# Four projections at the last super-block boundary over 512 columns in two contraction halves, and a later release of one buffer in the planner

## The chip, the cores and the metric

The kernel runs on one core of a Trainium2 chip. The metric is device time in microseconds (us), lower is better; every time below is of that one core. The engines are PE (TensorE, matmuls; PEld is its weight load), DVE (VectorE), ACT (ScalarE), POOL (GpSimd) and SP (SyncE, which here issues nearly all DMAs).

## The reference

One step of a layer that mixes attention and a gated linear recurrence, for 2048 prompt rows and 64 sample rows of width 1024, all in float32:

```
xn = rms_norm(x, ln_g)                                  # 2112 rows x 1024
aq, ak, av, ag, hq, hf, hi, hg = split(xn @ w_in)       # w_in 1024 x 4096: 8 parts of 512
o_a = band_attention(aq, ak, av) * silu(ag)             # 8 heads of 64, chunks of 64 rows, 576 keys each
o_b, S = hgrn2(hq, hf, hi, lb, state)                   # 4 heads of 128, blocks of 16 rows
o_b = rms_norm(o_b, norm_g) * silu(hg)
y = rms_norm(x + concat(o_a, o_b) @ w_out, ln_f_g)      # also returned: new keys, values and states
```

## The kernel before, in words

The rows are worked in four **super-blocks** (`sb` 0 to 3) of 512, 576, 512 and 512 rows. For each, the normalized rows stand transposed in SBUF, as a high part `xh` and a low part `xl` (both of the reduced float32 form that PE takes at its fast rate), 8 tiles `kt` of the contraction by the block's columns. There is one such pair of tiles; the next super-block's rows overwrite it.

A super-block has 32 **jobs** (`JOBS`), numbered `u` within it and `j` over all: one 128-column group of `w_in` each (`hf`, `hq`, `hi`, `hg` of a recurrent head, `pg`, `pq`, `pk`, `pv` of a pair of attention heads). `project` does one: 24 matmuls per range of columns (high x high, high weight x low, low weight x high, each over 8 `kt`) into one of two PSUM banks `acc`. A generator `evac` then empties the bank on ACT and DVE. The weight pair `w` (4 buffers) comes from a copy in DRAM, `wd`.

**The boundary.** Between two super-blocks PE must go on while `xh` and `xl` are rewritten. So the last two jobs of a super-block, and the first two of the next, are done in halves of 256 columns: job, job, on columns 0 to 255, then both on 256 to 511. After the first half the flag `x_left[sb, 0]` is set, after the second `x_left[sb, 1]`. The threads `x_back` (one per 128 rows) wait for the flag of their half of the columns, then write `xh` (an ACT cast for each half `k0` of the contraction, line 468) and spawn `x_low`, which writes `xl` (a DVE subtraction, line 474). The rows come from DRAM, already normalized and transposed, into a tile `xn` or `wraw`. `x_ready` tells the projections of the next super-block what has been written.

The values of attention, projected by `pv`, go from `acc` through a DVE block transpose (line 767), four DMAs to DRAM (`way<-vT`, line 787) and one back (`vT<-way`, line 791), then an ACT cast and a DVE subtraction into `v` (lines 756 and 759).

**The order.** One class, `Plan`, runs the whole kernel as generators at build time. It holds a clock `C.now` that the matmuls move on, and a free time for each engine; each buffer is a token (`tk[...]`), and `put(n, t)` says from what planned time it counts as free. A thread goes on when its token and its time have come, and instructions are written in the order in which threads go on. That order is then fixed on each engine. A planned time that is too early does no harm to the data: the instruction waits on the chip, and everything behind it on its engine waits too.

**The output part.** After the jobs the output projection runs as seven products per two tiles of rows (`steps`). `out_parts` splits each operand into a high part (ACT, line 1918) and a low part (DVE, or POOL at line 1926) in one of five rooms, the `slot`s. One room is made of `ob` and `gg`, the tiles of the recurrence's last output. It may be written once the store of `ob` to DRAM (`mixd<-ob`, line 1750, in `rec_block`) has read it. The last lines of `rec_block` say when the plan believes that:

```
sp.dma_start(mixd[sb][4 + h, :, c], ob[:, :bn])
if lastb and (sb, h) == (len(SUPER) - 1, NHB - 1):
    tk["slot"].put(1, C.now + 4500.0)
```

In attention, PE transposes the probabilities into one of two PSUM banks `tr` (line 254), ACT copies the high part `ph` (line 1055), DVE subtracts for the low part (line 1058), which frees the bank, and PE multiplies with the values into `pv`.

Of the kernel before, what the change touches and what calls it, by code (L numbers as in the profile page):

```python
# [19 lines left out]
KT = D // P  # L20
# [22 lines left out]
]  # L43
NMAX = 576


JOBS = [[(k, g) for g in range(4) for k in ("hf", "hq", "hi", "hg", "pg", "pq", "pk", "pv")] for _ in SUPER]
# [137 lines left out]
def hymba_step(  # L185
# [38 lines left out]
    C = Plan()  # L224
# [9 lines left out]
    def acc_ps():  # L234
        return psum("acc", bufs=2)
# [13 lines left out]
    def mm(out, w, x, n, slow=False, **kw):  # L249
        pe.matmul(out, w, x, **kw)  # L250
        C.mm(n, slow)

    def transpose(out, x, idn):
# [4 lines left out]
                                     w=WBUFS, raw=RAWB, xn=XNB, kv0=1, kv1=1, rec=1, sga=2, bias0=1, bias1=1, gf=1, gi=1, gg=1,  # L258
# [67 lines left out]
    xh = T(px, [P, KT, NMAX], F32R, "xh")  # L326
    xl = T(px, [P, KT, NMAX], F32R, "xl")

# [123 lines left out]
    def x_back(sb, half, c, rows, room, t):  # L452
        yield lambda: job[0] >= (20 if sb < 3 else 24) and x_turned.get(sb, 0) == c // P
        yield t
        while not (tk["xn"].n or tk["raw"].n):
            yield min(tk["xn"].when(), tk["raw"].when(), C.now + 300.0)
        tag = "xn" if tk["xn"].n else "raw"
        tk[tag].take()
        x_turned[sb] = c // P + 1
        xn = T(px, [P, D], F32, "xn", bufs=XNB) if tag == "xn" else raw_tile().rearrange("p k n -> p (k n)")  # L460
        sp.dma_start(xn[:, : 8 * rows], room.rearrange("p a x -> p (a x)"))
        t = C.dma(512 * rows / P) + 1000.0
        src = xn[:, : 8 * rows].rearrange("p (a k i) -> p k a i", k=KT, i=32)
        hi, lo = (x[:, :, c : c + rows].rearrange("p k (a i) -> p k a i", i=32) for x in (xh, xl))
        for k0 in (0, 4):
            yield lambda: x_left.get((sb - 1, half), False)
            yield "A", t
            act.copy(hi[:, k0 : k0 + 4], src[:, k0 : k0 + 4])
            C.spawn(x_low(sb, half, k0, rows, hi, lo, src, tag, C.act(4 * rows, t)), 0)
# [31 lines left out]
    def x_ready(sb, half, part, k0):  # L501
        tiles = (SUPER[sb][3][half][1] + P - 1) // P
        n, t = x_there.get((sb, half, part, k0), (0, 0.0))
        return n == tiles and t <= C.now
# [57 lines left out]
    def out_weights():  # L562


        for a in range(4):
            for tag in ("raw", "raw", "xn", "xn"):
                yield from tk[tag].get()
            r0, r1 = (raw_tile().rearrange("p k n -> p (k n)") for _ in range(2))
            stage = [T(px, [P, D], F32, "xn", bufs=XNB) for _ in range(2)]
            sp.dma_start(r0, w_out[a * P : (a + 1) * P, :])  # L570
            sp.dma_start(r1, w_out[(a + 4) * P : (a + 5) * P, :])
            yield "A", C.dma(1024)
            b11, b12, b21, b22 = r0[:, :512], r0[:, 512:], r1[:, :512], r1[:, 512:]
            state = dict(n=0, t=C.now)
            cols = [slice(c, c + 256) for c in (0, 256)]

            def split(i, src):
                st = stage[state["n"] % 2]
                t = max(state["t"], state.get(state["n"] - 2, 0.0))
                state["n"] += 1  # L580
                for c in cols:
                    yield "A", t
                    act.copy(f32r(st[:, c]), src[:, c])  # L583
                    t = C.act(256, t)
                    yield "P", t
                    pool.tensor_sub(f32r(st[:, c.start + 512 : c.stop + 512]), src[:, c], st[:, c])  # L586
                    t = C.pool(320, t)
                sp.dma_start(wod[i][:, :, a], st.rearrange("p (h c) -> p h c", h=2))
                state["t"] = t
                state[state["n"] - 1] = C.dma(512, t) + 2000.0  # L590

            def minus(out, x, y):
                for c in cols:
                    yield "P", state["t"]
                    pool.tensor_sub(out[:, c], x[:, c], y[:, c])
                    state["t"] = C.pool(320, state["t"])

            yield from split(0, b11)
            yield from split(1, b21)
            yield from split(5, b22)  # L600
            yield from tk["ck"].get()
            t3 = T(wk, [P, 512], F32, "ck", bufs=1)
            yield from minus(t3, b22, b12)
            yield from split(4, t3)
            tk["ck"].put(1, state["t"])
            yield from minus(b12, b12, b11)
            yield from minus(b22, b22, b12)
            yield from minus(b21, b21, b22)
            for i, src in ((3, b12), (2, b22), (6, b21)):
                yield from split(i, src)  # L610
            for tag, n in (("raw", 2), ("xn", 2)):
                tk[tag].put(n, C.now + 4000.0)
            yield C.now + 6000.0

    def project(j, ranges, evac, close=True, ready=None):
        yield lambda: j in w_at
        w, th, tl = w_at[j]
        yield th
        if ready:
            yield lambda: ready(0, 0)  # L620
        for off, bn in ranges:
            yield from tk["acc"].get()
            acc = acc_ps()
            n = 0
            for i, (wi, x) in enumerate(((0, xh), (0, xl), (1, xh))):
                for kt in range(KT):
                    if i == 2 and kt % 2 == 0:
                        yield lambda: len(tl) > kt // 2
                        yield tl[kt // 2]
                    if ready and i < 2 and kt % 4 == 0:  # L630
                        yield lambda: ready(i, kt)
                    mm(acc[:, :bn], w[:, wi, kt, :], x[:, kt, off : off + bn], bn,
                       start=(kt == 0 and i == 0), stop=(kt == KT - 1 and i == 2))
                    n += 1
                    if n % 2 == 0:
                        yield None
            C.spawn(evac(acc[:, :bn], off, bn, C.pe()), 0)
        if close:
            tk["w"].put(1, C.pe())
# [832 lines left out]
    def rec_block(r, off, bn, lastb):  # L1472
# [276 lines left out]
        yield t  # L1749
        sp.dma_start(mixd[sb][4 + h, :, c], ob[:, :bn])  # L1750
        if lastb and (sb, h) == (len(SUPER) - 1, NHB - 1):
            tk["slot"].put(1, C.now + 4500.0)
        done_g[sb, h] = done_g.get((sb, h), 0) + bn


# [422 lines left out]
    def program():  # L2178
# [67 lines left out]
        for sb in range(nsb):  # L2246
            last = sb == nsb - 1
            halves = SUPER[sb][3]
            blocks = SUPER[sb][2]
            if sb == 2:  # L2250
                C.spawn(out_weights(), 0.7)
            made = {}
            for u, (kind, g) in enumerate(JOBS[sb]):
                job[:] = u, sb
                if u == len(JOBS[sb]) - (8 if last else 32):
                    if last:
                        C.spawn(out_load(0), 1.5)
                        C.spawn(out_load(1), 1.6)
                        for rows in (out_rows_w(), out_rows_g(), out_rows_x(), out_rows_a()):
                            C.spawn(rows, 2)  # L2260
                    else:
                        C.spawn(x_turn(sb + 1), 0.5)
                if (kind[0], g) not in made:
                    d, evs = made[kind[0], g] = (head_jobs if kind[0] == "h" else pair_jobs)(sb, g)
                    C.spawn((recurrence if kind[0] == "h" else attention)(d), 1)
                evac = made[kind[0], g][1][kind[1]]

                if u == 1 or (u == len(JOBS[sb]) - 1 and not last):
                    for half in range(2):
                        yield from project(j - 1, [halves[half]], before, half == 1,  # L2270
                                           lambda part, k0: x_ready(sb, half, part, k0))
                        yield from project(j, [halves[half]], evac, half == 1,
                                           lambda part, k0: x_ready(sb, half, part, k0))
                        if u > 1:
                            x_left[sb, half] = True
                elif u != 0 and (last or u != len(JOBS[sb]) - 2):
                    yield from project(j, blocks, evac)
                    if u == len(JOBS[sb]) - 1:
                        x_left[sb, 0] = x_left[sb, 1] = True
                before = evac  # L2280
                j += 1
# [166 lines left out]
```

## Time and profile before

| what | value |
|---|---|
| median of 3 runs | 1211.92 us (1209.15 to 1214.72) |
| the profiled execution | 1212.41 us, of which 1210.4 us are the profile's span |
| mean granted PE clock | 0.997 |
| PE busy | 1195.2 us (99%), 7796 matmuls |
| PEld busy | 1051.3 us (87%) |
| DVE busy | 899.9 us (74%) |
| ACT busy | 715.0 us (59%) |
| POOL busy | 438.6 us (36%) |

The page names PE as busy for nearly the whole span, and 82% of the chain that ended last is PE. Matmuls are pipelined and the profile models their ends, so a matmul's duration is longer than the distance to the next; the distance between starts is what one costs. The boundary that the change touches lies at about 757 to 788 us; the store of the recurrence's last output at 1003 to 1009 us.

### The profile page before, as it was taken

Reading aid. Unit: us, or ns where it says so; the run is one execution under the profiler, and the core shown is the slowest. Engines: PE = TensorE matmul, PEld = TensorE weight load, DVE = VectorE, ACT = ScalarE, POOL = GpSimd, SP = SyncE. Lnnn points to the kernel's source line nnn. Section 1 sums busy time; section 2 is a strip of 40 time slices with the busy share of each in tenths; the row PEclk is TensorE's granted clock in tenths of the full one; section 3 lists DMA queues with packets and bytes.
Section 4 is the critical chain, followed back from the end, with each engine's and each line's share of the span. In section 5 each row is a group of like instructions: output and inputs, shape, how many; then the busy total and the mean of one; then the engine's idle time right before and its main releaser. Section 6 shows DMA issues by size and latency. Waiting matters only on the chain.

```text
span 1210.4 us, 22192 instructions
## 1 busy us (share of the span) xinstructions
PE 1195.2 (99%) x7796; PEld 1051.3 (87%) x7796; DVE 899.9 (74%) x1891; ACT 715.0 (59%) x1584; POOL 438.6 (36%) x738
## 2 busy tenths in 40 slices
PE   9999999999999999999999999999999998999997
PEld 7888788999999999998888888988888887888786
DVE  7698978777858777687677876786757574877775
ACT  6464655656666565774656665756656563644443
POOL 7776656112121121200234341143331213465443
PEclk9999999999999999999999999999999999999999
DMA  9899989687566595578697998688986677787431
GB/s 349 315 354 326 321 302 363 227 252 245 180 196 210 179 307 159 189 263 278 207 328 245 304 317 297 213 282 287 284 300 226 205 256 238 297 293 212 144 126 69
DMA packets 164696, 306.87 MB, mean 254 GB/s; under 512 B 49705, under 2 KB 102697, under 8 KB 146922
## 3 DMA queue, kind: packets, MB, share of 16 engines
q1 hardware_dynamic: 164152, 305.20, 74.5%
q8 instruction: 61, 1.00, 0.3%
q14 instruction: 49, 0.40, 0.1%
q10 hardware_dynamic: 434, 0.27, 0.1%
HBM read 204.75 MB, written 101.71 MB: 253 GB/s over the span
## 4 chain that ended last, share of the span: by engine, by line
PE 82%; DMA 5%; DVE 5%; ACT 4%; SPq 2%; issue 1%; POOL 1%; ACTq 0%; DVEq 0%; POOLq 0%
PE acc L250 53%; PE pv L250 7%; PE g L250 6%; PE s L250 5%; PE tr L254 5%; PE tr L250 4%; DMA xn<-in_x_prompt_dram 1%; DMA wraw<-in_w_in_dram 1%; PE g L1468 1%; SPq L445 1%; DMA carry<-kd 1%; DMA far<-in_rel_bias_dram 0%; DMA mixd<-ob 0%; ACT q L878 0%; DMA xn<-xt 0%
## 5 line engine op out<-in xcount | busy, mean ns | idle before, releaser
L250 PE MATMUL acc<-xh,w 128*128 128x512 f32 (+2 forms) x2720 | 564.1, 347 | 1.2 <-DVE sga L656 0.6
L250 PEld LDWEIGHTS acc<-xh,w 128*128 128x128 f32 x2720 | 436.2, 189 | 52.7 <-DVE sga L656 1.5
L250 PE MATMUL acc<-xl,w 128*128 128x512 f32 (+2 forms) x1360 | 290.8, 346 | 0.5 <-DVE xl L491 0.5
L250 PEld LDWEIGHTS acc<-xl,w 128*128 128x128 f32 x1360 | 220.5, 189 | 25.2 <-DVE xl L491 0.7
L1055 ACT CAST ph<-tr 128x512 fp32r<-128x512 f32 (+3 forms) x176 | 88.0, 507 | 72.4 <-PE pv L250 33.3
L1058 DVE TENSOR_TENSOR ph<-tr,ph 128x512 fp32r<-128x512 f32 (+3 forms) x176 | 101.3, 588 | 36.1 <-ACT ph L1055 35.3
L1043 ACT ACTIVATE pr<-pr,nm 128x640 f32<-128x640 f32 (+4 forms) x132 | 100.4, 761 | 36.8 <-DVE nm L1026 34.2
L1026 DVE CUSTOM_DVE_ANT_0 pr<-s,bias 128x640 f32<-128x640 f32 (+4 forms) x128 | 94.0, 734 | 36.4 <-PE s L250 35.4
L549 POOL TENSOR_TENSOR w<-wraw,w 128x256 fp32r<-128x256 f32 x120 | 105.6, 908 | 36.6 <-DVE w L544 16.2
L250 PE MATMUL pv<-ph,v 128*128 128x256 f32 (+2 forms) x344 | 96.6, 367 | 0.0
L254 PE MATMUL tr<-ident,pr 128*128 128x128 f32 x580 | 88.1, 272 | 3.5 <-DVE ph L1058 3.5
L1047 DVE TENSOR_SCALAR pr<-pr,sm 128x640 f32<-128x640 f32 (+4 forms) x132 | 80.7, 611 | 4.7
L254 PEld LDWEIGHTS tr<-ident,pr 128*128 128x128 f32 x580 | 70.1, 140 | 14.0 <-DVE ph L1058 3.9
L1097 DVE TENSOR_TENSOR mixa<-mixa,pv 64x256 f32<-64x256 f32 (+1 forms) x144 | 56.6, 393 | 31.7 <-ACT mixa L1093 28.5
L586 POOL TENSOR_TENSOR xn<-wraw,xn 128x256 fp32r<-128x256 f32 x48 | 39.5, 825 | 97.8 <-ACT xn L583 96.4
L1717 POOL TENSOR_TENSOR k<-k,q 64x512 f32<-64x512 f32 (+2 forms) x20 | 21.9, 1092 | 134.9 <-ACT q L1714 132.1
L1199 POOL TENSOR_TENSOR mixa<-mixa,sga 128x256 f32<-128x256 f32 (+1 forms) x36 | 30.9, 859 | 104.7 <-DVE mixa L1097 100.6
L250 PEld LDWEIGHTS pv<-ph,v 128*128 128x128 f32 x344 | 59.9, 190 | 7.8
L651 ACT ACTIVATE sig<-acc 128x512 f32<-128x512 f32 (+2 forms) x63 | 31.9, 506 | 55.5 <-PE acc L250 50.0
L1093 ACT COPY mixa<-pv 64x256 f32<-64x256 f32 (+1 forms) x72 | 25.2, 350 | 57.4 <-PE pv L250 55.5
L250 PE MATMUL s<-kd,q 128*128 128x320 f32 (+2 forms) x232 | 56.5, 313 | 1.3 <-DVE nm L1026 1.2
L1745 POOL TENSOR_TENSOR ob<-ob,gg 128x512 f32<-128x512 f32 (+2 forms) x20 | 24.5, 1225 | 88.7 <-DVE ob L1739 88.1
(553 smaller groups left out, 2163.9 us busy)
## 6 DMA issues: line engine op xcount, KB each, us to landing
w<-wd SPq DMA_DIRECT2D x96, 1024.0 KB, 6.2
wd<-w SPq DMA_DIRECT2D x32, 1024.0 KB, 8.2
wraw<-in_w_in_dram SPq DMA_DIRECT2D x30, 512.0 KB, 5.6
wod<-xn SPq DMA_DIRECT2D x28, 512.0 KB, 5.3
xn<-in_x_prompt_dram SPq DMA_DIRECT2D x23, 512.0 KB, 6.5
bias<-biasd SPq DMA_DIRECT2D x24, 320.0 KB, 5.7
xt<-xn SPq DMA_DIRECT2D x50, 128.0 KB, 5.4
carry<-kd SPq DMA_DIRECT2D x12, 512.0 KB, 5.8
```

Source lines behind the costliest of these rows:

```text
L250: pe.matmul(out, w, x, **kw)
L254: pe.transpose(out, x, idn)
L549: pool.tensor_sub(w[:, 1, k : k + 2], raw[:, k : k + 2], f32(w[:, 0, k : k + 2]))
L586: pool.tensor_sub(f32r(st[:, c.start + 512 : c.stop + 512]), src[:, c], st[:, c])
L651: act.activation(sig[:, :bn], acc, AF.Exp, scale=-1.0)
L1026: dve.tensor_tensor_reduce(s[:, :nk].rearrange("p (a c) -> p a c", a=ns), sps[:, :ns, :kn], d.bias[:, h, bcol : bcol + nk].rearrange("p (a ...
L1043: act.activation(s[:, :nk], s[:, :nk], AF.Exp, bias=nm[:, 0:1], scale=-1.0, accum_out=sm)
L1047: dve.tensor_scalar(s[:, :nk], s[:, :nk], sm, None, ALU.mult)
L1055: act.copy(ph[:krows, 0, :wid], pt[:krows, :wid])
L1058: dve.tensor_sub(ph[:krows, 1, :wid], pt[:krows, :wid], f32(ph[:krows, 0, :wid]))
L1097: dve.tensor_add(mix[hs, :qn], mix[hs, :qn], pv[hs, i, :qn])
L1199: pool.tensor_mul(mix[:, :n], mix[:, :n], d.sg[:, g0 : g0 + n])
```

## The change

At the boundary from super-block 2 to 3 (`KT_BOUND = (2,)`) the two last and the two first jobs no longer run on halves of the columns. A new function `project_kt` takes both jobs together and all 512 columns, and halves the contraction: `kt` 0 to 3 of the first job, of the second, then `kt` 4 to 7 of the first, of the second. Each job holds its `acc` bank from its first half to its second. The flag `x_left[2, 0]` now says that `kt` 0 to 3 of all columns are no longer needed, `x_left[2, 1]` the same of `kt` 4 to 7, and `x_back` asks for the flag of the half of the contraction that it writes. The other boundaries stay as they were.

The second edit is one number: the room of `ob` and `gg` counts in the plan as free 9000 ns after its store is written, where it was 4500 ns.

```diff
+KT_BOUND = (2,)
...
         for k0 in (0, 4):
-            yield lambda: x_left.get((sb - 1, half), False)
+            yield lambda: x_left.get((sb - 1, k0 // 4 if sb - 1 in KT_BOUND else half), False)
             yield "A", t
             act.copy(hi[:, k0 : k0 + 4], src[:, k0 : k0 + 4])
...
+    def project_kt(js, ranges, sb, ready=None):
+        for j, _ in js:
+            yield lambda: j in w_at
+            yield w_at[j][1]
+        accs = {}
+        for k0 in (0, 4):
+            for j, evac in js:
+                w = w_at[j][0]
+                for off, bn in ranges:
+                    if k0 == 0:
+                        yield from tk["acc"].get()
+                        accs[j, off] = acc_ps()
+                for i, (wi, x) in enumerate(((0, xh), (1, xh), (0, xl))):
+                    if ready and i != 1:
+                        yield lambda: ready(i // 2, k0)
+                    for kt in range(k0, k0 + 4):
+                        for off, bn in ranges:
+                            mm(accs[j, off][:, :bn], w[:, wi, kt, :], x[:, kt, off : off + bn], bn,
+                               start=(kt == 0 and i == 0), stop=(kt == KT - 1 and i == 2))
+                        if kt % 2 or len(ranges) > 1:
+                            yield None
+                if k0:
+                    for off, bn in ranges:
+                        C.spawn(evac(accs[j, off][:, :bn], off, bn, C.pe()), 0)
+                    tk["w"].put(1, C.pe())
+            if not ready:
+                x_left[sb, k0 // 4] = True
...
         if lastb and (sb, h) == (len(SUPER) - 1, NHB - 1):
-            tk["slot"].put(1, C.now + 4500.0)
+            tk["slot"].put(1, C.now + 9000.0)
...
-                if u == 1 or (u == len(JOBS[sb]) - 1 and not last):
+                both = [(j - 1, before), (j, evac)] if u else [(j, evac)]
+                if sb in KT_BOUND and u == len(JOBS[sb]) - 1:
+                    yield from project_kt(both, blocks, sb)
+                elif sb - 1 in KT_BOUND and u == len(blocks) % 2:
+                    yield from project_kt(both, blocks, sb,
+                                          lambda part, k0: all(x_ready(sb, i, part, k0) for i in range(2)))
+                elif sb - 1 in KT_BOUND and len(blocks) == 2 and u == 1:
+                    yield from project(j, blocks, evac)
+                elif u == 1 or (u == len(JOBS[sb]) - 1 and not last):
```

**PE at the boundary.** The names in a row are out<-in; `acc` is a job's PSUM bank, `w` its weights, `tr`, `pv` and `s` are attention's, `g` the recurrence's; "x4" at the end counts equal instructions. Before, the second-to-last job of super-block 2 on columns 0 to 255 (`acc_9945`), the start of the last one (`acc_9994`), and further on both again on columns 256 to 511:

```order
L250 MATMUL acc_9945<-xh_156,w_9655 128x256 x4
L254 MATMUL tr_9954<-ident_69,pr_9772 128x128
L254 MATMUL tr_9954<-ident_69,pr_9809 128x128
L250 MATMUL acc_9945<-xh_156,w_9655 128x256 x4
L250 MATMUL acc_9945<-xl_157,w_9655 128x256 x6
L250 MATMUL pv_9974<-ph_9930,v_585 128x512 x2
L250 MATMUL acc_9945<-xl_157,w_9655 128x256 x2
L250 MATMUL acc_9945<-xh_156,w_9655 128x256 x8
L250 MATMUL acc_9994<-xh_156,w_9764 128x256 x2
```

Now, at the same place: both jobs over 512 columns, `kt` 0 to 3 of `acc_9945`, of `acc_9982`, and the first two of `kt` 4 to 7:

```order
L251 MATMUL acc_9945<-xh_156,w_9655 128x512 x2
L255 MATMUL tr_9952<-ident_69,pr_9772 128x128
L255 MATMUL tr_9952<-ident_69,pr_9809 128x128
L251 MATMUL acc_9945<-xh_156,w_9655 128x512 x6
L251 MATMUL pv_9968<-ph_9930,v_585 128x512 x2
L251 MATMUL acc_9945<-xl_157,w_9655 128x512 x4
L251 MATMUL acc_9982<-xh_156,w_9764 128x512 x4
L251 MATMUL g_9987<-gi_9759,k_1883_9975 128x128 x4
L251 MATMUL pv_9968<-ph_9950,v_585 128x512 x2
L251 MATMUL acc_9982<-xh_156,w_9764 128x512 x4
L251 MATMUL acc_9982<-xl_157,w_9764 128x512 x4
L251 MATMUL acc_9945<-xh_156,w_9655 128x512 x2
```

Over the whole kernel 192 matmuls of 256 columns become 96 of 512, and nothing else on PE changes in number; the small work between them stands in another order from here to about the middle of super-block 3.

**ACT at the room of `ob`.** Before, the cast that fills the room (`ob_12852`) stands ahead of two casts of attention's probabilities (`ph`) and a copy:

```order
L916 COPY vT_12835<-acc_12717 128x512
L1055 CAST ph_12837<-tr_12800 128x256
L1918 CAST ob_12852<-xn_12302 128x512
L1055 CAST ph_12859<-tr_12844 128x512
L1093 COPY mixa_12557<-pv_12828 64x256
L1055 CAST ph_12876<-tr_12866 128x512
L1055 CAST ph_12899<-tr_12882 128x256
```

Now it (`ob_12763`) stands behind those three, and ahead of the third cast of that unit of attention:

```order
L945 COPY vT_12704<-acc_12586 128x512
L1084 CAST ph_12706<-tr_12669 128x256
L1084 CAST ph_12725<-tr_12713 128x512
L1122 COPY mixa_12426<-pv_12697 64x256
L1084 CAST ph_12741<-tr_12732 128x512
L1947 CAST ob_12763<-xn_12171 128x512
L1084 CAST ph_12766<-tr_12747 128x256
```

**PE at the same place.** Now, the transposes into `tr_12747` and what follows them; before, the same instructions stood there, with 2 instead of 4 matmuls of the next job (the one after `acc_12701`) ahead of the last `pv`:

```order
L251 MATMUL acc_12701<-xl_157,w_12301 128x512 x4
L255 MATMUL tr_12747<-ident_69,pr_12619 128x128
L255 MATMUL tr_12747<-ident_69,pr_12650 128x128
L251 MATMUL acc_12701<-xl_157,w_12301 128x512 x4
L251 MATMUL acc_12701<-xh_156,w_12301 128x512 x2
L251 MATMUL pv_12758<-ph_12725,v_585 128x512 x2
L251 MATMUL pv_12758<-ph_12741,v_585 128x512 x2
L251 MATMUL acc_12701<-xh_156,w_12301 128x512 x6
L251 MATMUL acc_12777<-xh_156,w_12474 128x512 x4
L251 MATMUL pv_12758<-ph_12766,v_585 128x2x128 x2
```

The transposes into `tr_12747` reuse the bank of `tr_12713`, which the DVE subtraction behind the cast `ph_12725` frees; that cast has moved ahead of the cast into `ob`. Only the last `pv` needs a cast that still stands behind it.

## The prediction

> **What bounds the kernel now.** I read the page first, then PE's waits, then PE's timeline at both places that the change touches, and last the queues behind the one long wait.
>
> ```profile
> span 1210.4 us, 22192 instructions
> PE 1195.2 (99%) x7796; PEld 1051.3 (87%) x7796; DVE 899.9 (74%) x1891; ACT 715.0 (59%) x1584; POOL 438.6 (36%) x738
> ...
> PE tr L254 <- DVE ph L1058: 3.5, 1, 3.5
> ```
>
> PE is busy all through. So a change gains only by fewer PE microseconds or by a PE wait that goes, and loses only where PE gets a new wait. The third line is the longest wait of PE in the whole run; it happens once, here (start, duration, what):
>
> ```profile
> 1006.45 1.17 PE L250 MATMUL acc<-xl,w 128*128 128x512 f32 x4
> 1011.13 0.51 PE L254 MATMUL tr<-ident,pr 128*128 128x128 f32 x2 [3.51 <-DVE ph L1058]
> 1011.32 2.03 PE L250 MATMUL acc<-xl,w 128*128 128x512 f32 x4
> 1013.15 1.05 PE L250 MATMUL acc<-xh,w 128*128 128x512 f32 x2
> 1014.00 1.45 PE L250 MATMUL pv<-ph,v 128*128 128x512 f32 x4
> 1015.29 2.01 PE L250 MATMUL acc<-xh,w 128*128 128x512 f32 x8
> 1017.14 0.39 PE L250 MATMUL pv<-ph,v 128*128 128x256 f32 x2
> ...
> 1011.00:1013.00 2.00, 1.87 (x6) 1.58 (x7) 1.61 (x4) 0.35 (x1) 1.08 (x2) 0.59 0.00 0
> 1013.00:1015.30 2.30, 2.30 (x8) 1.76 (x8) 0.00 (x0) 0.28 (x1) 0.00 (x0) 0.62 0.21 64
> 1015.30:1018.00 2.70, 2.70 (x14) 2.27 (x13) 0.45 (x2) 1.10 (x4) 0.00 (x0) 1.00 0.91 282
> ```
>
> The number after the busy times is the granted clock: 0.59 and 0.62 behind the wait, 1.00 only from about 1015.3. Four matmuls that take 0.9 us at full clock take 1.83 us at 1011.32. The wait is therefore paid twice. Its cause is on ACT and SP:
>
> ```profile
> 999.91 3.32 SPq L522 DMA_DIRECT2D w<-wd  x1
> 1003.33 0.38 SPq L1750 DMA_DIRECT2D mixd<-ob  x1
> ...
> 1003.38 0.37 ACT L1055 CAST ph<-tr 128x256 fp32r<-128x256 f32 x1
> 1009.25 0.62 ACT L1918 CAST ob<-xn 128x512 fp32r<-128x512 f32 x1 [5.50 <-DMA mixd<-ob]
> 1009.77 0.58 ACT L1055 CAST ph<-tr 128x512 fp32r<-128x512 f32 x1
> 1010.38 0.36 ACT L1093 COPY mixa<-pv 64x256 f32<-64x256 f32 x1
> 1010.76 0.59 ACT L1055 CAST ph<-tr 128x512 fp32r<-128x512 f32 x1
> 1015.02 0.37 ACT L1055 CAST ph<-tr 128x256 fp32r<-128x256 f32 x1 [3.67 <-PE pv L250]
> ```
>
> The store of `ob` stands on SP behind a weight load that waits, so it is issued only at 1003.33 and is read out at 1009.25, 5.9 us later. ACT sits at the cast into `ob` for 5.50 us, with two `ph` casts behind it that PE needs.
>
> **The price of a matmul.** Distances between starts, in stretches without other work, for 512 columns and for 256:
>
> ```profile
> 672.12 3.79 PE L250 MATMUL acc<-xh,w 128*128 128x512 f32 x16
> 675.75 1.98 PE L250 MATMUL acc<-xl,w 128*128 128x512 f32 x8
> ...
> 770.19 2.08 PE L250 MATMUL acc<-xh,w 128*128 128x256 f32 x16
> 772.11 1.12 PE L250 MATMUL acc<-xl,w 128*128 128x256 f32 x8
> 773.07 1.84 PE L250 MATMUL acc<-xh,w 128*128 128x256 f32 x14
> ...
> 757.23:788.27 31.04, 31.04 (x254) 30.74 (x253) 24.49 (x53) 24.03 (x53) 4.02 (x4) 1.00 0.65 226
> ```
>
> 512 columns: (675.75 - 672.12) / 16 = 0.227 us. 256 columns: (772.11 - 770.19) / 16 = 0.120, and 0.96 / 8 = 0.120 again. Half a matmul costs more than half, but only by 0.0066 us. The last row is the boundary's 31.04 us: PE 31.04 busy, no wait to be had, so the gain here is that difference and no more.
>
> **The change part by part.**
>
> 1. Halves of the contraction. 192 matmuls of 256 columns go, 96 of 512 come: 192 x 0.120 = 23.04 us against 96 x 0.227 = 21.79, a gain of 1.25 us. Against it, PE's new order leaves the transposes 166 times instead of 162, and each leaving costs some time:
>
> ```profile
> 667.12 1.03 PE L254 MATMUL tr<-ident,pr 128*128 128x128 f32 x8
> 667.91 2.56 PE L250 MATMUL acc<-xh,w 128*128 128x512 f32 x10
> 670.31 1.98 PE L250 MATMUL acc<-xl,w 128*128 128x512 f32 x8
> ```
>
> Ten matmuls behind transposes take 2.40 us, 0.13 above 10 x 0.227. Four more leavings are 0.5 us. Net gain 0.75; ends 0 and 1.3.
>
> 2. The new waits at the boundary, costed at nothing with this cover. The rewriting works in two lots of four ACT casts and four DVE subtractions:
>
> ```profile
> 766.83 0.36 ACT L1093 COPY mixa<-pv 64x256 f32<-64x256 f32 x1 [4.96 <-PE pv L250]
> 770.41 0.40 ACT L899 CAST kd<-vT 64x256 fp32r<-64x256 f32 x1
> 770.83 1.66 ACT L468 CAST xh<-xn 128x512 fp32r<-128x512 f32 x3
> 772.20 2.50 DVE L474 TENSOR_TENSOR xl<-xn,xh 128x512 fp32r<-128x512 f32 x4
> ...
> 775.09 2.18 SPq L787 DMA_DIRECT2D way<-vT  x4
> 782.09 0.33 SPq L791 DMA_DIRECT2D vT<-way  x1
> 789.89 0.29 ACT L756 CAST v<-vT 128x128 fp32r<-128x128 f32 x1
> ```
>
> At 0.55 us a cast and 0.62 a subtraction a lot is written about 3.5 us after PE has left it. PE meanwhile has 24 matmuls of the other half of the contraction, 24 x 0.227 = 5.4 us, and needs the low part later still by eight matmuls. Slack 2 to 4 us; without cover a lot would cost up to 3.5. The two `acc` banks are now held through both halves: the next super-block's first job needs the first bank 12 matmuls (2.7 us) after it is complete, and the copy that empties it stands behind the run of ACT work that starts at 766.83, when a `pv` is done, and lasts to 770.41, 3.6 us. In the new order ten matmuls (2.3 us) lie between that `pv` and the bank's completion, so 1.3 us of the run are left and then the copy, about 0.6. Slack 0.8 us, the thinnest. The weights of both jobs are released within 2.7 us of each other, at 12 matmuls before the end and at the end, which is no later than now. Four DMAs out and one back for the values replace twice as many half-size ones, and start only when the whole last job is done: in the rows above this way takes 14.8 us (775.09 to 789.89). PE first needs these values 80 matmuls (18.2 us) and eight transposes (0.8, priced from the rows of part 1) after the last job, so 19 us at the least. The order after that changes as far as the middle of super-block 3, without a row that PE would wait for in the trace of before. I take 0; ends 0 and +4 us.
>
> 3. The room of `ob`. ACT does two `ph` casts and the `mixa` copy ahead of the cast into `ob`. What PE loses now: from 1006.45 to 1017.14 is 10.69 us; in it stand 22 matmuls of 512 columns (5.0 us) and two transposes with their leaving (0.3), so 5.3 us at full clock. The loss is 5.4 us: about 3.8 of standing still and 1.6 of half clock. With the new order PE runs on: transposes at 1007.4, the 512-column `pv` at 1009.1 and 1009.5 (their casts are done by 1007.2), ten more matmuls to 1012.2, and then the last `pv`, whose cast now stands behind `ob`. The store lands at 1009.25 as before, since the SP rows ahead of it are the same; cast into `ob` to 1009.8, `ph` to 1010.2, its DVE subtraction to 1010.6. That leaves 1.6 us of slack, and no wait. POOL's low part of that room moves behind one `mixa` product; the product that reads the room comes some 30 us later:
>
> ```profile
> 1042.04 0.39 PE L250 MATMUL g<-w,ob 128*128 128x512 f32 x1
> ...
> w<-wod SPq DMA_DIRECT2D x4, 1024.0 KB, 8.5
> ```
>
> That far ahead, a later fill costs nothing. I take the whole 5.4; ends 0 and 5.4.
>
> The Trainium skill ("TensorE: Matmul & The Clock Gate", Part 1: The HAM clock gate) says that the clock falls to half after an idle window of about 3.4 us, that the window runs freely, and that the clock comes back after a busy window. The rows agree as far as they go: 3.8 us of idleness, then clocks of 0.59 and 0.62 for about 4 us. By that rule the idle stretch is barely longer than the window, so in some executions of the old kernel the clock part (1.6 of the 5.4) may not be lost, and the gain would be 4.5 instead of 6.1.
>
> **The sum** against the profiled execution's own 1212.41 us: -5.4 - 1.25 + 0.5 = -6.15, which gives 1206.3 us. The median shown, 1211.92, is 0.5 us lower; against it the gain is 5.6 us, 0.46%. A half per cent (6.06 us) is about what a measurement of this kernel can tell from no change: the three runs alone lie 5.6 us apart. So a forecast of a real gain stands just at that bound.
>
> **The rivals.**
>
> - The wait is only shortened. The store's 5.9 us are those of one execution; if it lands later than 1.6 us after 1009.25, PE waits at the last `pv`. For it: SP issues it behind a waiting load, and the larger loads of that stretch take 8.5 us to land (the row just above). Against it: a wait of one or two us would not bring the clock down. Price at 3 us of delay: 1.4 us, 1207.7.
> - The second edit does not do what it says: the cast moves three rows, but ACT still blocks a row that PE needs at once. Then the 5.4 stays and the first edit alone counts: 1211.7. Against it: the only `ph` cast behind `ob` is needed 4.8 us later than the transposes that wait now.
> - The boundary's cover is too thin: a bank or a half of `xh` comes late, or the new order of super-block 3 meets a wait on a DMA, as the one for `ob` was. 1 to 4 us: 1207.3 to 1210.3. For it: DVE is busy for 24.5 of the 31 us at the boundary, and its order changes most. Against it: none of PE's waits lies there now.
> - Slower: the values of the last pair. SP now has two loads of `w_out` (which wait for the last subtraction from their room) and a store of `kd` ahead of `vT<-way`, and all 512 columns hang on that one transfer. It becomes the bound once it is more than 19 - 14.8 = 4 us late. It makes the kernel slower once PE stands for more than 4.6 us, since such a wait also costs the half clock (1.6 us as above), so from 9 us of delay; at 12 us the time is 1206.3 + 8 + 1.6 = 1216.
>
> **How the numbers follow.** Both edits as summed: 0.56, with its own spread of 1.5 us about 1206.3 from the ends of part 1 and from runs. Wait shortened only: 0.11. Second edit without effect: 0.08. A new wait of 1 to 4 us: 0.20. The values late and slower: 0.05. The range holds the first two, most of the new waits and part of the third case: 1203.6 to 1211.5. Faster by over 0.5% means below 1205.9: somewhat under half of the first case, and the case that the boundary's gain is whole and the order does better than counted; 0.37. Slower by over 0.5% (above 1218.0): the far end of the last case, 0.04. The rest, 0.59, is within 0.5%.
>
> **What would show it.** In the new profile PE has no wait of over 1 us on `ph` near the store of `ob`, and the granted clock stays at 1.00 there. ACT's wait for that store is shorter (some 2 us), and it stands behind two `ph` casts. The boundary between super-blocks 2 and 3 is PE without a gap, with matmuls at 0.227 us. PE's waits by line show nothing of `acc` on `xh` or `xl` above 0.5 us. The prediction is wrong if PE waits at the first jobs of super-block 3 or at the `pv` there, or if the wait for `ob` returns at the last `pv`.

## The result, and the profile after

| kernel | median of its runs | lowest to highest |
|---|---|---|
| before | 1211.92 us (7 runs) | 1209.15 to 1215.58 |
| changed | 1205.19 us (7 runs) | 1203.45 to 1207.12 |

The ratio of the runs is 0.9939, 95% interval 0.9923 to 0.9955: 0.61% less, between 0.45 and 0.77% (the two medians lie 0.56% apart). The forecast was 1206.3 us with a range of 1203.6 to 1211.5. The profiled execution took 1207.12 us, 1205.4 of them the span. Page and PE's waits of the changed kernel (engine, line and tile, what it waited for: us in total, times, longest):

```profile
span 1205.4 us, 21978 instructions
PE 1191.4 (99%) x7700; PEld 1043.0 (87%) x7700; DVE 896.3 (74%) x1882; ACT 712.7 (59%) x1572; POOL 436.2 (36%) x738
...
PE pv L2257 <- POOL one L281: 1.4, 1, 1.4
PE s L251 <- DVE nm L1055: 1.2, 3, 0.7
PE acc L251 <- DVE sm L1075: 0.9, 1, 0.9
```

PE has 96 matmuls fewer, as counted, and the row of 3.5 us on `ph` is gone. The longest wait left is the one at the start of the kernel. PE's timeline at the store of `ob`, then the same stretch by engines (window, its length, busy us of PE, PEld, DVE, ACT, POOL with counts, granted clock, DMA share, GB/s):

```profile
1006.13 0.40 PE L251 MATMUL pv<-ph,v 128*128 128x256 f32 x2
...
1006.72 1.17 PE L251 MATMUL acc<-xl,w 128*128 128x512 f32 x4
1007.72 0.38 PE L255 MATMUL tr<-ident,pr 128*128 128x128 f32 x2
1007.86 1.16 PE L251 MATMUL acc<-xl,w 128*128 128x512 f32 x4
...
1009.31 1.09 PE L251 MATMUL pv<-ph,v 128*128 128x512 f32 x4
1010.23 2.44 PE L251 MATMUL acc<-xh,w 128*128 128x512 f32 x10
1012.51 0.40 PE L251 MATMUL pv<-ph,v 128*128 128x256 f32 x2
...
1009.00:1012.90 3.90, 3.90 (x20) 3.24 (x19) 0.43 (x1) 1.60 (x4) 1.43 (x2) 1.00 0.93 302
```

The transposes of 1007.72 carry no bracket: PE did not wait for them. Four matmuls that took 1.83 us now take 1.0, and the clock is 1.00. ACT and SP at the same place:

```profile
1002.53 0.38 SPq L1779 DMA_DIRECT2D mixd<-ob  x1
...
1007.00 0.59 ACT L1084 CAST ph<-tr 128x512 fp32r<-128x512 f32 x1
1008.54 0.62 ACT L1947 CAST ob<-xn 128x512 fp32r<-128x512 f32 x1 [0.96 <-DMA mixd<-ob]
1009.96 0.37 ACT L1084 CAST ph<-tr 128x256 fp32r<-128x256 f32 x1 [0.80 <-PE pv L251]
```

The store still takes 6.0 us from issue to reading out (1002.53 to 1008.54), but ACT now loses 0.96 us to it instead of 5.50, with one `ph` cast behind it. That cast waits for PE, not for `ob`.

Now the boundary, by engines and then by rows of PE, ACT and DVE:

```profile
758.38:788.54 30.16, 30.16 (x157) 25.55 (x156) 21.08 (x40) 20.57 (x40) 4.93 (x5) 1.00 0.74 243
...
770.83 1.98 PE L251 MATMUL acc<-xh,w 128*128 128x512 f32 x8
772.65 1.07 PE L251 MATMUL acc<-xl,w 128*128 128x512 f32 x4
773.55 1.98 PE L251 MATMUL acc<-xh,w 128*128 128x512 f32 x8
...
782.25 1.08 PE L251 MATMUL acc<-xl,w 128*128 128x512 f32 x4
...
772.20 0.57 ACT L921 COPY vT<-acc 128x512 f32<-128x512 f32 x1
...
777.03 0.68 DVE L475 TENSOR_TENSOR xl<-wraw,xh 128x512 fp32r<-128x512 f32 x1
```

No gap on PE. The copy that empties the first bank ends at 772.77, and PE writes that bank again at 773.55: 0.78 us of slack. The low part of the second lot is written by 777.71 and first read at 782.25, 4.5 us later.

**One measure for all the runs.** PE does the same work up to the boundary in before, in the changed kernel and in all variants but one, yet the boundary starts anywhere between 754.77 and 760.62 us, since small waits in the first 280 us differ from execution to execution (the wait on `sm` at 257 us is 0.34 us before and 0.94 after). So I compare two later stretches: A from the first matmul of the boundary's jobs to the `pv` of 256 columns ahead of the old wait, B from there to the end of the span.

| kernel | A starts | A ends | A | B | 
|---|---|---|---|---|
| before | 757.23 | 1005.86 | 248.63 | 204.54 |
| changed | 758.38 | 1006.13 | 247.75 | 199.27 |
| room only | 756.24 | 1004.88 | 248.64 | 199.22 |
| halves only | 757.51 | 1005.16 | 247.65 | 204.94 |
| room, 6000 ns | 760.62 | 1009.26 | 248.64 | 199.24 |
| room, 20000 ns | 754.77 | 1002.40 | 247.63 | 199.30 |
| no halving | 757.54 | 1011.27 | 253.73 | 199.33 |
| store from ACT | 755.41 | 1005.45 | 250.04 | 201.35 |

A is 248.63 or 248.64 us in three kernels without the halves of the contraction and 247.63 to 247.75 in the three that have them: 0.9 to 1.0 us less. B is 199.22 to 199.33 us wherever the room counts as free later, and 204.54 and 204.94 in the two kernels where it does not and the store goes out as in before: 5.2 to 5.7 us less. So the two edits do not touch one another. The last two rows of the table have waits of their own, told below; the variant that is not in the table is the one whose order differs from the first boundary on.

### The profile page after: what moved, and what is told of

It is laid out like the page before. It is cut to its first block, busy times and chain, and to the rows that moved or that the text cites. A ratio compares the mean times of both kernels' runs of the same rounds, so it can differ in the third digit from the quotient of the medians.

```text
span 1205.4 us, 21978 instructions
## 1 busy us (share of the span) xinstructions
PE 1191.4 (99%) x7700; PEld 1043.0 (87%) x7700; DVE 896.3 (74%) x1882; ACT 712.7 (59%) x1572; POOL 436.2 (36%) x738
## 4 chain that ended last, share of the span: by engine, by line
PE 85%; DVE 4%; DMA 4%; ACT 3%; SPq 2%; issue 1%; POOL 1%; DVEq 0%; ACTq 0%
PE acc L251 55%; PE pv L251 7%; PE g L251 6%; PE s L251 6%; PE tr L255 5%; PE tr L251 4%; PE g L1497 1%; SPq L446 1%; DMA carry<-v 1%; DMA xn<-in_x_prompt_dram 1%; DMA w<-wd 1%; DMA far<-in_rel_bias_dram 0%; POOL w L550 0%; DMA wraw<-in_w_in_dram 0%; DVE w L545 0%
## 5 line engine op out<-in xcount | busy, mean ns | idle before, releaser
L251 PEld LDWEIGHTS acc<-xh,w 128*128 128x128 f32 x2656 | 431.0, 189 | 55.8 <-DVE sga L685 1.5
L251 PEld LDWEIGHTS acc<-xl,w 128*128 128x128 f32 x1328 | 217.8, 189 | 26.9 <-DVE xl L492 0.9
L251 PE MATMUL s<-kd,ql 128*128 128x320 f32 (+2 forms) x232 | 55.5, 309 | 0.0
```

## The experiments

Seven variants ran, in two groups, each group on one chip beside the kernel before: 1212.88 us there for the first four below, 1212.27 for the last three. Ratios are to before.

**The second edit alone** (`e1_room_only`).

```diff
-KT_BOUND = (2,)
+KT_BOUND = ()
```

> Only the second edit: the room counts as free 9000 ns after the store, all boundaries in column halves as before. Theory (the wait for the store of ob with the half clock behind it is nearly the whole gain): 5.4 us less than before, about 1206.6; in the trace no PE wait over 1 us between 1000 and 1020 us and a granted clock of 1.00 there. Rival (the boundary carries a larger part than its matmuls' price says): less than 4 us gained here.

1207.69 us, ratio 0.9956 (0.9940 to 0.9972), 5.3 us less by the ratio. PE and ACT at the store:

```profile
1004.88 0.40 PE L251 MATMUL pv<-ph,v 128*128 128x256 f32 x2
...
1006.47 0.38 PE L255 MATMUL tr<-ident,pr 128*128 128x128 f32 x2
...
1011.26 0.40 PE L251 MATMUL pv<-ph,v 128*128 128x256 f32 x2
...
1008.22 0.62 ACT L1947 CAST ob<-xn 128x512 fp32r<-128x512 f32 x1 [1.89 <-DMA mixd<-ob]
```

From `pv` to `pv` it is 6.38 us, where before it was 11.28 (1005.86 to 1017.14, with two matmuls less). The store came 3.34 us after the first `pv`, as late as before (3.39), and PE still did not wait. So the gain does not come from an earlier store.

**The first edit alone** (`e2_halves_only`).

```diff
-            tk["slot"].put(1, C.now + 9000.0)
+            tk["slot"].put(1, C.now + 4500.0)
```

> Only the first edit: contraction halves at the last boundary, the room free after 4500 ns as before. Theory: 0.75 us less than before (ends 0 and 1.3), about 1211.2, the wait for ob of some 3.5 us on PE still there with a clock of about 0.6 behind it. Rival (the boundary carries more than its matmuls' price): 2 to 3 us less.

1210.61 us, ratio 0.9988 (0.9974 to 1.0001). Its interval holds no change and 3 us alike, so for this term the runs decide nothing. The traces do, by stretch A of the three kernels with and the three without the halves. The old wait is there, with its clock:

```profile
1010.90 0.69 PE L255 MATMUL tr<-ident,pr 128*128 128x128 f32 x2 [3.98 <-DVE ph L1087]
...
1006.90:1010.90 4.00, 0.02 (x2) 0.01 (x1) 0.72 (x2) 1.84 (x4) 1.19 (x2) 0.97 0.76 297
1010.90:1013.00 2.10, 2.10 (x6) 1.81 (x7) 1.51 (x3) 0.21 (x1) 0.95 (x2) 0.50 0.00 0
1013.00:1015.00 2.00, 2.00 (x8) 1.54 (x7) 0.00 (x0) 0.31 (x1) 0.00 (x0) 0.72 0.66 147
```

**The room at 6000 ns** (`e7_room_6us`): one `ph` cast less ahead of the cast into `ob`, without the halves.

```diff
-KT_BOUND = (2,)
+KT_BOUND = ()
...
-            tk["slot"].put(1, C.now + 9000.0)
+            tk["slot"].put(1, C.now + 6000.0)
```

> Second edit alone with 6000 ns: the cast into ob stands behind one ph cast and the mixa copy, but ahead of the second ph cast. PE should run on through the transposes and the first pv and wait only at the second, from about 1009.5 to 1011: some 1.6 us. Theory (the half clock follows only a wait as long as the 3.8 us one): clock stays at 1.00, so 3.8 us less than before, about 1208.1. Rival (any wait here is followed by the half clock): 1.6 us more than that, about 1209.7.

1208.05 us, ratio 0.9967 (0.9956 to 0.9978): 4.0 us less, close to the 3.8 expected. But that is no proof of the theory, since the profile does not show the 1.6 us wait that the 3.8 was worked out from:

```profile
1009.26 0.40 PE L251 MATMUL pv<-ph,v 128*128 128x256 f32 x2
...
1010.85 0.38 PE L255 MATMUL tr<-ident,pr 128*128 128x128 f32 x2
...
1010.95 0.62 ACT L1947 CAST ob<-xn 128x512 fp32r<-128x512 f32 x1 [0.90 <-DMA mixd<-ob]
```

Here the store was read out 1.69 us after the `pv`; in before it was 3.39, in the changed kernel 2.41, with the halves alone 3.85. So it floats by 2.2 us against PE over the traces in which ACT waits for it, and this one lies at the early end. Nearly all of that is in the issue, which comes 2.24 to 4.17 us ahead of the `pv` in the same traces; from issue to landing the store takes 5.5 to 5.9 us wherever it goes out from SP and the trace tells it. The issue itself follows another transfer: in the eight traces that tell when the 1 MB load `b11l<-wod`, issued some 11 to 12 us before the store, has landed, the weight load `w<-wd` that the store stands behind leaves SP's queue 0.1 to 0.2 us before that (in before at 1003.23 and 1003.37).

The mean granted clock was 0.999 in 9 of this kernel's 12 executions and in none of the 30 of before beside it, which fits a half clock that is gone. Whether the 1.3 us between the gains by the two ratios, here and at 9000 ns, are waits in the other executions stays open: the two intervals overlap.

**The store sooner instead of the cast later** (`e5_act_store`): the plan's number stays at 4500, the halves are out, and the store is issued from ACT's queue, so that it does not stand behind SP's weight load.

```diff
-        sp.dma_start(mixd[sb][4 + h, :, c], ob[:, :bn])
+        (act if lastb and (sb, h) == (len(SUPER) - 1, NHB - 1) else sp).dma_start(mixd[sb][4 + h, :, c], ob[:, :bn])
```

> Neither edit; instead the last store of ob is issued from ACT's queue and not from SP's, the cast into ob stands where it stood before. Theory (the store lands late because it stands on SP behind a weight load that waits; it is issued at 1003.3, some 4 us after its data): it is issued at about 1000 us and lands at about 1005.5, ACT waits some 2 us, PE not or under 1 us, no half clock: 5 us less than before, about 1207. Rival (the transfer itself is slow whenever it starts, because other transfers are ahead of it): it lands near 1009 again and nothing is gained.

1211.84 us, ratio 0.9987 (0.9975 to 1.0000): a miss, 1.6 us instead of 5.

```profile
995.86 1.30 POOL L1774 TENSOR_TENSOR ob<-ob,gg 128x512 f32<-128x512 f32 x1 [3.56 <-DVE ob L1768]
...
1000.57 0.34 ACTq L1779 DMA_DIRECT2D mixd<-ob  x1
1000.95 0.83 ACT L1072 ACTIVATE pr<-pr,nm 128x640 f32<-128x640 f32 x1 [2.50 <-DMA b11l<-wod]
...
1007.30 0.62 ACT L1947 CAST ob<-xn 128x512 fp32r<-128x512 f32 x1 [4.05 <-DMA mixd<-ob]
...
1003.56 0.66 PE L255 MATMUL tr<-ident,pr 128*128 128x128 f32 x4 [1.17 <-DVE ph L1087]
...
1009.18 0.44 PE L255 MATMUL tr<-ident,pr 128*128 128x128 f32 x2 [1.97 <-DVE ph L1087]
...
1009.18:1011.00 1.82, 1.82 (x9) 1.56 (x10) 1.52 (x3) 0.21 (x1) 0.95 (x2) 1.00 0.00 0
```

The issue is earlier (4.9 us ahead of the `pv`, in before 2.5) and comes about when it was expected. But the store then takes 6.7 us instead of 5.9, and ACT itself stood 2.50 us around the issue behind a load of weights (`b11l<-wod`), which gives PE a wait of its own, 1.17 us. So A is 1.4 us longer than in before, and B only 3.2 shorter. The profiled execution is the fastest of the twelve (1208.79 us), so the waits may be longer in others.

The wait on that load comes with the edit. The data was ready at 997.16, when the POOL row ends. In the trace's records the store and that load signal their landing by the same semaphore (number 110), and ACT waits for it before it issues the store; on SP the store of before has another number (107). So this variant shows that moving the store to ACT's queue, as it was done here, does not pay. What a store would give that is issued as soon as its data is ready was not tried. The Trainium skill ("DMA: Bandwidth & Descriptors", section Queues, rings and completion order) says that the queues of SP and ACT are rings on the same 16 engines. The trace agrees as far as it goes: another queue brought the issue forward by 2.4 us against the `pv`, and the transfer was no shorter, 6.7 us.

**The last boundary without any halving** (`e3_whole`): both jobs one after the other on all columns and the whole contraction, with the room at 9000 ns.

```diff
-                    yield from project_kt(both, blocks, sb)
+                    for jj, ev in both:
+                        yield from project(jj, blocks, ev)
+                    x_left[sb, 0] = x_left[sb, 1] = True
...
-                    yield from project_kt(both, blocks, sb,
-                                          lambda part, k0: all(x_ready(sb, i, part, k0) for i in range(2)))
+                    for jj, ev in both:
+                        yield from project(jj, blocks, ev, True,
+                                           lambda part, k0: all(x_ready(sb, i, part, k0) for i in range(2)))
```

> Last boundary without any halving: both jobs on all 512 columns and the whole contraction, one after the other, and the room of ob at 9000 ns. The same 96 matmuls of 512 columns as in the new kernel, but the rewriting of xh and xl can start only when the last job is done. Theory (the halves of the contraction are the cover of the rewriting): PE stands for about one lot, 3.5 us, less what other PE work lies there, at the first job of super-block 3 with ACT or DVE of xh or xl named, and perhaps 1.6 us more by a half clock behind it; 3 to 6 us slower than the new kernel, 1208.2 to 1211.2. Rival (attention and the recurrence are cover enough, and the halving is worth only its matmul price): within 1 us of the new kernel, and no wait of PE over 1 us at the boundary.

1211.34 us, ratio 0.9988 (0.9972 to 1.0005): the theory, 5.5 us above the variant with 20000 ns on the same chip, which equals the changed kernel.

```profile
774.48 0.45 PE L251 MATMUL s<-kd,ql 128*128 128x320 f32 x2
777.39 3.68 PE L251 MATMUL acc<-xh,w 128*128 128x512 f32 x8 [2.46 <-ACT xh L469]
780.91 1.55 PE L251 MATMUL acc<-xl,w 128*128 128x512 f32 x6
...
774.90:777.39 2.49, 0.04 (x1) 0.00 (x0) 2.49 (x5) 2.49 (x6) 0.00 (x0) 1.00 0.93 204
777.39:779.20 1.81, 1.81 (x4) 1.49 (x5) 1.81 (x4) 1.30 (x3) 0.00 (x0) 0.51 0.93 272
779.20:781.00 1.80, 1.80 (x6) 1.40 (x5) 1.74 (x4) 0.00 (x0) 0.00 (x0) 0.55 0.99 364
...
876.41 0.69 PE L251 MATMUL pv<-ph,v 128*128 128x512 f32 x2 [1.15 <-DVE sm L1075]
```

PE stands 2.46 us for the rewriting, then eight matmuls take 3.52 us (777.39 to 780.91) instead of 1.82. With the wait on `sm` a hundred us later that makes 5.3 of the 6.0 us by which stretch A is longer than in the changed kernel. So wider matmuls alone lose here: A is 5.1 us longer than with the halves of the columns (248.64, room only). What pays is that the halves of the contraction keep the cover that the halves of the columns gave.

**The same at the first boundary too** (`e4_two_bounds`).

```diff
-KT_BOUND = (2,)
+KT_BOUND = (0, 2)
```

> The halves of the contraction at the first boundary as well (super-block 1 has two ranges of columns, so its first job there takes both acc banks), the room of ob at 9000 ns. Theory (the gain is the price of the matmuls): some 0.5 to 1 us less than the new kernel, 1204.2 to 1204.7, and no PE wait on acc there. Rival (a boundary is only worth its change where each job needs one bank): with both banks held by one job PE waits for their copies, 0.6 to 3 us; 0 to 3 us slower than the new kernel, 1205.2 to 1208.2, with acc named in PE's waits in the first half of the run.

1207.71 us, ratio 0.9969 (0.9956 to 0.9981): the rival, 1.9 us above the 20000 ns variant on the same chip (its twelve runs start at 1206.72, the six of the other end at 1206.91). PE has 48 matmuls less, but:

```profile
233.01 0.28 PE L251 MATMUL acc<-xh,w 128*128 128x256 f32 x1
234.27 2.25 PE L251 MATMUL acc<-xh,w 128*128 128x320 f32 x15 [0.98 <-DVE vT L796]
...
233.40 0.72 DVE L796 STREAM_TRANSPOSE vT<-acc 128x512 f32<-128x512 f32 x1
...
555.57 0.65 PE L255 MATMUL tr<-ident,pr 128*128 128x128 f32 x4 [0.98 <-DVE ph L1087]
```

The first job of super-block 1 has two ranges and so needs both banks. The second bank is the one that the last job of super-block 0 has just filled, and PE waits 0.98 us for the transpose that empties it. It is the same kind of slack as the thinnest of the forecast, the bank's 0.8 us at the last boundary, here turned into a wait. Another 0.98 us stands at 555.57, and 0.43 us at 510.15, where the order has shifted. The three make 2.4 us, enough for the 1.9 us and the gain that did not come; one trace does not tell it closer.

**The room at 20000 ns** (`e6_room_20us`), with the halves.

```diff
-            tk["slot"].put(1, C.now + 9000.0)
+            tk["slot"].put(1, C.now + 20000.0)
```

> The new kernel with the room of ob counted as free 20000 ns after its store instead of 9000. The cast into ob then stands behind all three ph casts of that unit. Theory (the gain of the second edit is whole: no PE wait is left there to take away, and the product that reads the room comes some 30 us later): the same as the new kernel within 0.5 us, 1205.2; ACT's wait for the store falls from 0.96 us to nothing. Rival 1 (in executions other than the profiled one the store still makes the last ph cast late): 0.5 to 1.5 us faster than the new kernel. Rival 2 (a later filling delays the output products): PE waits with ob named, 1 us or more slower.

1205.83 us, ratio 0.9949 (0.9932 to 0.9967): the same as the changed kernel (0.9939). B is 199.30 against 199.27 us. The last `ph` cast of that unit no longer stands behind `ob`:

```profile
1003.27 0.59 ACT L1084 CAST ph<-tr 128x512 fp32r<-128x512 f32 x1
1006.24 0.37 ACT L1084 CAST ph<-tr 128x256 fp32r<-128x256 f32 x1 [2.38 <-PE pv L251]
```

There was nothing left to gain at this place. No variant beats the changed kernel by its ratio to before.

## Why the prediction was right

- **What bounds the kernel.** Right: the whole gain lies in PE's own microseconds and in the one PE wait that went. From the start of the boundary to the end the span fell by 6.15 us (453.17 to 447.02), which is the sum worked out. That it fits to the hundredth is luck: the two terms came as 0.88 and 5.27 us where 0.75 and 5.4 were forecast.
- **Halves of the contraction, 0.75 us forecast.** 0.88 between the traces of before and after, up to 1.01 over the other pairs of kernels with and without them. The price of a matmul holds: 16 of 512 columns take 3.63 us in the new trace as well (791.73 to 795.36), 0.227 each. The 0.5 us for four more leavings of the transposes was too much: of the 1.25 us for the matmuls, 0.24 to 0.37 did not come.
- **The boundary's cover, costed at nothing.** Right, and the slack named as the thinnest, the `acc` bank's 0.8 us, measured 0.78. The conversions had as much as the 2 to 4 us given, or a little more: 4.1 for the last high part (an ACT cast, written by 775.50 and first read at 779.60), 4.5 for the last low part. The values' way took 16.3 us to its first cast (774.50 to 790.78) instead of 14.8, and PE did not wait for it.
- **The room of `ob`, 5.4 us forecast.** 5.27 between the traces, 5.3 by the runs of that edit alone. Of its two halves, 3.8 of standing and 1.6 of half clock, the second can be measured: the half clock lasts 3.4 us in three traces, which costs 1.7. Whether the old kernel lost it in every execution stays open. Of the 30 executions of before beside the first four variants, the 8 with a mean clock of 0.998 took 1.5 us less on average than the 12 with 0.997 (1210.68 and 1212.19), as they would without it, but no trace of them was kept.
- **"A wait of one or two us would not bring the clock down."** At 1.97 us it did not (clock 1.00 behind it, store from ACT); at 2.46 us it did (0.51 and 0.55, no halving). So a wait well short of the 3.8 us can bring it down, and the rival of a new wait of 1 to 4 us, priced without the half clock, was priced up to 1.7 us too low. What more can be said of the line stands in the last section.
- **The wait only shortened.** Did not come: the last `ph` cast started at 1009.96, 0.8 us after the cast into `ob` had ended, and what it waited for was a `pv` of PE. The forecast had the store land as late as before, and here it was read out 1.0 us earlier against PE, which is luck. The gain does not hang on it: in the second edit alone the store came as late as before, the last `ph` cast went right behind `ob` (1008.74, its subtraction done by 1009.56), and the `pv` at 1011.26 had 1.7 us of slack, where 1.6 was forecast.
- **Second edit without effect, the values late.** Neither came.

The weak point is the chances. Most of the weight went to a change within 0.5%, because 5.6 us against the median shown was taken as just under the bound. Medians of seven runs lie 6.7 us apart, and by the ratio the gain is 0.61%: its centre fell on the other side of that bound, though the interval of 0.45 to 0.77% still holds it. The step was the 0.5 us by which the first median lay under the profiled execution: medians of three groups of runs of before spread over 1.0 us (1211.92 to 1212.88), so such a difference says nothing of the change.

## What to carry to other kernels

When PE is busy all through, look for the one long wait and follow it past the engine that is named: here PE named DVE, DVE's cast stood on ACT, ACT on a store, and the store on SP's queue. The cheap cure was to put the cast behind other ready work. The one try to hurry the store did not pay, since it made ACT wait for another transfer. When one splits work to cover a rewriting, there is a choice of which dimension to split: the contraction keeps the matmuls wide, but it holds the accumulator banks longer, so the number of banks that a job needs can decide whether it pays. And an order fixed from planned times should leave room for how a transfer's end floats, 2.2 us here.

## What the runs showed of the hardware

- The half clock comes behind a shorter wait than I had thought. Waits of 2.46, 3.51 and 3.98 us were followed by it, one of 1.97 us was not. It then lasted the same time each time, 3.41 us: 1011.36 to 1014.77 in before, 1010.69 to 1014.10 with the halves alone, 777.41 to 780.83 without halving, at 0.50. The Trainium skill ("TensorE: Matmul & The Clock Gate", Part 1: The HAM clock gate) names a free-running window of about 3.4 us, and the length agrees. So does the running: in the clock records of all nine traces the stretches at full clock are whole multiples of 3.413 us long (293 and 56 of them in before). Its rule that the clock falls after an idle window does not fit as it stands. These are the windows on that grid that hold the most of the wait, of before, of the variant without halving, and of the one with the store from ACT:

```profile
1007.94:1011.36 3.42, 0.23 (x3) 0.23 (x3) 0.95 (x2) 2.05 (x4) 1.41 (x2) 1.00 0.75 293
774.00:777.41 3.41, 0.95 (x6) 0.61 (x5) 3.38 (x9) 3.35 (x8) 0.00 (x0) 1.00 0.69 154
1007.57:1010.98 3.41, 1.80 (x9) 1.55 (x10) 2.24 (x4) 1.78 (x4) 2.14 (x3) 1.00 0.07 27
```

  PE was busy for 0.23, 0.95 and 1.80 us of them. The first two were followed by the half clock, the third was not. So a window need not be idle throughout: 72% was enough here, 47% was not, and where a wait falls on the grid should then count beside its length. These are one trace each; no run tells where between the two the line is.
- Narrower matmuls are only a little dearer: two of 256 columns take 0.240 us, one of 512 takes 0.227. In this kernel that is 1.25 us for 96 of them.
- The store of `ob`, 256 KB, took 5.5 to 5.9 us from issue to landing in the traces that issued it from SP's queue, 6.7 in the one that issued it from ACT's.
